# The causal mask as a matmul that opens each score bank of a four-layer decoder trunk

## The chip, the cores and the metric

The kernel runs on one core of one Trainium2 chip. The metric is the device time of one execution in microseconds (us); lower is better. One matrix engine (PE, the TensorE), three elementwise engines (DVE = VectorE, ACT = ScalarE, POOL = GpSimd) and the queue that issues transfers (SP) work side by side and wait for each other through semaphores. Scores and products land in PSUM, which has eight banks of 128 partitions x 512 float32.

## The reference

A trunk of four residual layers over 256 tokens of width 1024, batch 1. Layers 0 and 3 mix tokens by native sparse attention (NSA), layer 1 by block attention (MoBA), layer 2 by a gated short convolution; each layer ends in a dense SwiGLU network, and a last norm follows. With 256 tokens the sparse rules leave plain causal attention in two of NSA's three branches and in MoBA:

```python
def masked_softmax(s, mask):
    s = jnp.where(mask, s.astype(jnp.float32), -jnp.inf)
    m = jnp.max(s, axis=-1, keepdims=True)
    m = jnp.where(jnp.isfinite(m), m, 0.0)
    e = jnp.where(mask, jnp.exp(s - m), 0.0)
    d = jnp.sum(e, axis=-1, keepdims=True)
    return e / jnp.where(d > 0, d, 1.0)
...
# NSA: 16 heads, the selected and the window branch share the mask kpos <= t
o = (gates[:, :, 0] * o_cmp + gates[:, :, 1] * o_slc + gates[:, :, 2] * o_win) @ w_out
# MoBA: 16 heads, one block of 256 keys, mask kpos <= t
o = (masked_softmax(q @ k.T / 8, causal) @ v) @ w_out
```

## The kernel before

Activations stand with the model's width on the partitions, 256 tokens in the free dimension. All products are made from two parts of each number (high and low, type float32r), three matmuls for one product (`mm3`, L123 to L125). The weights stream from memory in blocks of 128x1024; `split_part` turns each into its parts (L104 the high one, L105 the low one), on ACT, DVE and POOL by a table. A projection (`project`) gathers 24 matmuls of 256 columns in one PSUM bank, and `scaled` (L276, DVE) multiplies it by the norm's factors.

Attention works by pairs of heads, eight pairs to a layer; the order of its steps is written out by hand (`NSA_ORDER`, `MOBA_ORDER`): q and k/K project, s makes scores and softmax, T transposes the probabilities (PE against an identity, then `split` on ACT and DVE, L138 and L139), P weighs the values. The framework's planner takes that order as a priority, and places an instruction earlier where its inputs and buffers allow it; on each engine the planned order is then fixed. PSUM is shared out by tags: A has four banks (projections, scores, values, output products), B three, C one.

`scores` of NSA fills three A banks for a pair: one with the first 128 queries of both heads and both branches (four blocks of 128x128, L643), and one for each head with the second 128 queries (two blocks of 128x256, L646). MoBA fills two (L371 to L373: two blocks of 128x128, two of 128x256). `softmax` (L297 to L314) is called once for each head in NSA and once for each pair in MoBA, with four score blocks each: for each block one DVE instruction (L306) reads the scores from PSUM, adds the mask, scales, writes the result to the SBUF tile `pr` and keeps the row's minimum, and a small read of that accumulator follows; ACT takes the exponential in place in `pr` (L309) with the row's sum, again with a small accumulator read; DVE makes the reciprocal of four sums (L311); POOL scales each block (L313). `pr` tiles hold 768 columns, and there are four of them.

The mask is a constant tile of 128x256 that is loaded at the start (L772) on the SP queue, behind the input and the first four weight blocks.

Of the kernel before, what the change touches and what calls it, by code (L numbers as in the profile page):

```python
# [51 lines left out]
class Kernel:  # L52
# [67 lines left out]
    def mm3(self, out, wt, act, first, last):  # L120
        """out += wt.T @ act, both as (high, low)."""
        mm = self.nc.tensor.matmul
        mm(out, wt[0], act[0], start=first, stop=False)  # L123
        mm(out, wt[0], act[1], start=False, stop=False)  # L124
        mm(out, wt[1], act[0], start=False, stop=last)  # L125

    def group(self, outs, acts):
        """outs[i][128, 256] = (weight tiles i, i + len(outs), ...).T @ acts."""
        n = len(acts)
        for k, a in enumerate(acts):  # L130
            if k == n - 1 and self.sums is None:
# [10 lines left out]
    def prep(self, k, norm):  # L142
        """The k-th slice of the norm's input: its parts times the gain, and its squares."""
# [130 lines left out]
    def scaled(self, p):  # L274
        f = self.row()
        self.nc.vector.tensor_tensor(out=f, in0=p, in1=self.rb, op=OP.mult)  # L276
        return f

    def values(self, at, put):
        """Token-major values of 512 columns; put(token tile, bank)."""  # L280
# [16 lines left out]
    def softmax(self, cols, gates):  # L297
# [3 lines left out]
        mn = self.sb([P, 4], "mn", bufs=3)  # L301
        den = self.sb([P, 4], "den", bufs=3)
        rc = self.sb([P, 4], "rc", bufs=3)
# [21 lines left out]
    def put_keys(self, dst, p):  # L325
        """dst[:, part, half, :]: the keys of a pair of heads, each with zeros for the other's rows."""
        nc = self.nc
        f = self.scaled(p)
# [10 lines left out]
    def moba(self, norm):  # L339
# [24 lines left out]
        def scores(p):  # L364
            q, kt = qs[p], self.keys[p % 4]
            s = []
            for t in range(NT):
                n = (t + 1) * P
                o = self.bank("A")[:, :2 * n].rearrange("p (a s) -> p a s", a=2)
                c = slice(t * P, (t + 1) * P)  # L370
                mm(o, q[:, 0, c], kt[:, 0, :, :n], start=True, stop=False)  # L371
                mm(o, q[:, 1, c], kt[:, 0, :, :n], start=False, stop=False)
                mm(o, q[:, 0, c], kt[:, 1, :, :n], start=False, stop=True)  # L373
                s.append(o)
            cols = [(s[t][:, i], slice((t + i) * S if t else i * P, (t + i + 1) * S if t else (i + 1) * P))
                    for t in range(NT) for i in range(2)]
            prs.append(self.softmax(cols, [1.0] * 4))

        def turn(p):
            pr = prs[p]  # L380
            b0, b1 = self.bank("B"), self.bank("B")
            for i in range(2):
                nc.tensor.transpose(b0[:, i * S:i * S + P], pr[:, i * P:(i + 1) * P], self.ident)
                o = (1 + i) * S
                nc.tensor.transpose(b0[:, i * S + P:(i + 1) * S], pr[:, o:o + P], self.ident)
                nc.tensor.transpose(b1[:, i * P:(i + 1) * P], pr[:, o + P:o + S], self.ident)
# [27 lines left out]
    def nsa(self, j, norm):  # L414
# [7 lines left out]
        # Keys and values to compress: rows (l % 2, d), the lower half one token ahead.  # L422
# [18 lines left out]
        def put_blocks(n):  # L441
            """Parts of the blocks' rows l = 2 jj, 2 jj + 1; columns (part, group, block), the position as block 15."""
# [15 lines left out]
        # Keys of the other branches: kk[:, part, branch, :], each part on both halves.  # L458
        def put_keys(b, gp):
            def put(p):  # L460
                f = self.scaled(p)
# [21 lines left out]
        # Queries: per head high and low parts on the two halves.  # L483
# [19 lines left out]
        def compress(n):  # L503
            """Rows (part, group, block), columns hidden."""
# [34 lines left out]
        def compress_keys(_):  # L539
            """Compressed keys on both halves."""  # L540
# [8 lines left out]
        def compress_values(_):  # L549
            """Compressed values as rows (r, part, block), one block of rows for each head of a group."""  # L550
# [27 lines left out]
        def compressed(gp):  # L578
            """Probabilities of the compressed blocks for 8 heads, rows (r, part, block)."""
# [42 lines left out]
        def put_values(t, p):  # L622
            """Per branch and pair of groups: (group, high | low | high, d)."""
# [13 lines left out]
        def scores(p):  # L637
            kk = self.keys[p // 2]
            s0 = self.bank("A").rearrange("p (i b s) -> p i b s", i=2, b=2)
            s1 = [self.bank("A").rearrange("p (b s) -> p b s", b=2) for _ in range(2)]  # L640
            for i in range(2):
                for n in range(2):
                    mm(s0[:, i], qs[p][:, i, :P], kk[:, n, :, :P], start=(n == 0), stop=(n == 1))  # L643
# [3 lines left out]
            prs.append([])  # L647
            for i in range(2):
                cols = [(s0[:, i, b], slice(b * P, (b + 1) * P)) for b in range(2)]
                cols += [(s1[i][:, b], slice((1 + b) * S, (2 + b) * S)) for b in range(2)]  # L650
                h = 2 * p + i
                g = [gates[:, t, 16 * (b + 1) + h:16 * (b + 1) + h + 1] for t in range(2) for b in range(2)]
                prs[p].append(self.softmax(cols, g))
# [94 lines left out]
    def run(self):  # L748
# [23 lines left out]
        self.mask = load("mask", [P, S])  # L772
# [4 lines left out]
        make_identity(nc, self.ident)  # L777
        self.ones = const.tile([P, 1], F32, tag="ones", name="ones")
# [38 lines left out]
def wide_tiles(w, cols):  # L817
    """[K, cols] -> tiles ordered (k, column block)."""
# [4 lines left out]
def stream():  # L823
    """The weights in the order of use: (step, array, layer of its kind, columns or rows of them)."""
# [37 lines left out]
def tiles(x):  # L862
    """The stream as blocks of PART tiles side by side."""
# [12 lines left out]
def layout(x):  # L876
    t = np.arange(S)
    own = np.where(np.arange(P)[:, None] >= np.arange(P)[None, :], 0.0, NEG)
    mask = np.concatenate([np.zeros((P, P)), own], axis=1).astype(np.float32)
# [35 lines left out]
```

## Time and profile before

| what | us |
|---|---|
| median of three runs | 1336.04 |
| lowest and highest run | 1332.56, 1336.41 |
| span of the profiled execution, first to last instruction | 1335.3 |
| PE busy | 1275.1 |
| DVE busy | 958.5 |
| ACT busy | 680.1 |
| POOL busy | 322.1 |

The profile shows the span of its execution, and no time around it; the span is 0.7 us under the median of the runs. A busy time counts an engine's instructions from start to end, overlaps once; matmuls overlap, and a matmul's row is longer than its step to the next one.

### The profile page before, as it was taken

The numbers are of one execution on the slowest core, as the hardware profiler recorded it, in microseconds if no ns is written. First come the engines' busy times: TensorE is split into PE (matmuls) and PEld (weight loads), VectorE is DVE, ScalarE is ACT, GpSimd is POOL, SyncE is SP. The second block draws the span as 40 slices with busy tenths as digits, with TensorE's granted clock in tenths as the row PEclk, the third lists the DMA queues.
The fourth block names the chain that finished last, engine by engine and source line by source line (L and its number), as shares of the span: only waits on it lengthen the run. The fifth ranks groups of instructions, "written<-read, shape, count | busy, mean of one in ns | idle before, by whom it ended". The sixth has DMA issues, their size and how long they took to land.

```text
span 1335.3 us, 25478 instructions
## 1 busy us (share of the span) xinstructions
PE 1275.1 (95%) x10064; PEld 1239.5 (93%) x10064; DVE 958.5 (72%) x1726; ACT 680.1 (51%) x1297; POOL 322.1 (24%) x341
## 2 busy tenths in 40 slices
PE   7779999999999899999999999999997989999997
PEld 7778899999989899999999999999996779999997
DVE  7988877665658886666658777665679798766642
ACT  4759845444434545444434344444346796544442
POOL 5457630000256320000113120000333666000010
PEclk9889999999999999999999999999998899999999
DMA  6443066555554236656555556666546312656651
GB/s 225 150 160 111 18 190 187 179 187 184 179 175 152 101 122 195 180 184 187 177 189 173 191 174 190 178 186 187 178 142 213 103 48 77 193 183 182 188 178 60
DMA packets 60744, 215.52 MB, mean 161 GB/s; under 512 B 7248, under 2 KB 7632, under 8 KB 60624
## 3 DMA queue, kind: packets, MB, share of 16 engines
q1 hardware_dynamic: 60480, 213.85, 50.9%
q8 instruction: 79, 1.29, 0.4%
q14 instruction: 41, 0.34, 0.1%
q10 hardware_dynamic: 144, 0.04, 0.0%
HBM read 212.81 MB, written 1.05 MB: 160 GB/s over the span
## 4 chain that ended last, share of the span: by engine, by line
PE 78%; DVE 13%; ACT 4%; issue 3%; DMA 1%; POOL 0%; POOLq 0%; DVEq 0%; ACTq 0%
PE psA L123 22%; PE psA L124 22%; PE psA L125 22%; DVE wlo L105 2%; PE psB L123 2%; PE psB L124 2%; PE psB L125 2%; ACT pr L309 1%; DVE ff L139 1%; DVE pt L139 1%; DVE row L276 1%; PE psA L289 1%; DVE pr L306 1%; PE psA L290 1%; PE psA L291 1%
## 5 line engine op out<-in xcount | busy, mean ns | idle before, releaser
L105 DVE TENSOR_TENSOR wlo<-raw,whi 128x1024 fp32r<-128x1024 f32 (+1 forms) x351 | 430.8, 1231 | 186.4 <-ACT whi L104 185.4
L123 PE MATMUL psA<-at,whi 128*128 128x256 f32 x1896 | 541.6, 286 | 18.1 <-DVE row L276 11.4
L104 ACT CAST whi<-raw 128x1024 fp32r<-128x1024 f32 (+1 forms) x372 | 386.0, 1040 | 335.5 <-issue 131.8
L125 PE MATMUL psA<-at,wlo 128*128 128x256 f32 x1896 | 539.9, 285 | 4.7 <-DVE wlo L105 2.8
L124 PE MATMUL psA<-at,whi 128*128 128x256 f32 x1896 | 539.4, 284 | 0.0
L123 PEld LDWEIGHTS psA<-at,whi 128*128 128x128 f32 x1896 | 366.5, 193 | 19.8 <-ACT whi L104 7.2
L125 PEld LDWEIGHTS psA<-at,wlo 128*128 128x128 f32 x1896 | 366.5, 193 | 6.2 <-DVE wlo L105 4.2
L124 PEld LDWEIGHTS psA<-at,whi 128*128 128x128 f32 x1896 | 366.7, 193 | 0.4
L124 PE MATMUL psA<-ff,whi 128*128 128x256 f32 x840 | 236.7, 282 | 2.1 <-DVE ff L139 2.1
L123 PE MATMUL psA<-ff,whi 128*128 128x256 f32 x840 | 236.7, 282 | 0.0
L125 PE MATMUL psA<-ff,wlo 128*128 128x256 f32 x840 | 236.0, 282 | 0.0
L167 POOL TENSOR_TENSOR ssq<-ssq,row 128x256 f32<-128x256 f32 x54 | 54.8, 1015 | 592.8 <-issue 476.7
L124 PEld LDWEIGHTS psA<-ff,whi 128*128 128x128 f32 x840 | 158.2, 188 | 2.8 <-DVE ff L139 2.5
L123 PEld LDWEIGHTS psA<-ff,whi 128*128 128x128 f32 x840 | 158.1, 188 | 0.1
L125 PEld LDWEIGHTS psA<-ff,wlo 128*128 128x128 f32 x840 | 158.0, 188 | 0.0
L105 POOL TENSOR_TENSOR wlo<-raw,whi 128x1024 fp32r<-128x1024 f32 (+1 forms) x55 | 133.2, 2427 | 77.8 <-ACT whi L104 37.1
L138 ACT CAST ff<-row 128x256 fp32r<-128x256 f32 x120 | 48.8, 407 | 127.9 <-DVE row L245 96.1
L139 DVE TENSOR_TENSOR ff<-row,ff 128x256 fp32r<-128x256 f32 x120 | 65.1, 543 | 37.7 <-ACT ff L138 36.7
L269 DVE TENSOR_TENSOR gu<-psA,rb 128x512 f32<-128x512 f32 x80 | 55.2, 691 | 38.5 <-PE psA L125 38.4
L313 POOL TENSOR_SCALAR pr<-pr,rc,gates 128x256 f32<-128x256 f32 (+1 forms) x128 | 69.3, 556 | 40.5 <-DVE rc L311 33.1
L309 ACT ACTIVATE pr<-pr,mn 128x128 f32<-128x128 f32 (+1 forms) x160 | 71.3, 449 | 6.1 <-DVE mn L306 5.7
L165 ACT ACTIVATE row<-h 128x256 f32<-128x256 f32 x63 | 24.5, 413 | 68.9 <-DVE h L229 67.3
(192 smaller groups left out, 1582.8 us busy)
## 6 DMA issues: line engine op xcount, KB each, us to landing
raw<-in_w SPq DMA_DIRECT2D x400, 512.0 KB, 3.6
h<-in_xt SPq DMA_DIRECT2D x4, 256.0 KB, 5.1
raw<-in_w SPq DMA_DIRECT2D x4, 256.0 KB, 5.2
out<-ff SPq DMA_DIRECT2D x4, 256.0 KB, 2.5
w<-in_w SPq DMA_DIRECT2D x2, 256.0 KB, 4.3
mask<-in_mask SPq DMA_DIRECT2D x1, 128.0 KB, 7.0
cneg<-in_cneg SPq DMA_DIRECT2D x1, 128.0 KB, 6.7
cone<-in_cone SPq DMA_DIRECT2D x1, 128.0 KB, 5.7
```

Source lines behind the costliest of these rows:

```text
L104: copy(hi[:, c], src[:, c])
L105: eng.tensor_tensor(out=lo[:, c], in0=src[:, c], in1=hi[:, c].bitcast(F32), op=OP.subtract)
L123: mm(out, wt[0], act[0], start=first, stop=False)
L124: mm(out, wt[0], act[1], start=False, stop=False)
L125: mm(out, wt[1], act[0], start=False, stop=last)
L138: self.nc.scalar.copy(dst[:, 0], src)
L139: self.nc.vector.tensor_tensor(out=dst[:, 1], in0=src, in1=dst[:, 0].bitcast(F32), op=OP.subtract)
L165: nc.scalar.activation(sq, h, AF.Square)
L167: nc.gpsimd.tensor_tensor(out=self.ssq, in0=self.ssq, in1=sq, op=OP.add)
L269: nc.vector.tensor_tensor(out=gu, in0=p, in1=self.rb[:, None, :].to_broadcast([P, 2, S]), op=OP.mult)
L309: nc.scalar.activation(pr[:, c], pr[:, c], AF.Exp, bias=mn[:, j:j + 1], scale=-1.0, accum_out=den[:, j:j + 1])
L313: nc.gpsimd.tensor_scalar(pr[:, c], pr[:, c], rc[:, j:j + 1], gates[j], op0=OP.mult, op1=OP.mult)
```

## The change

The mask tile becomes 128x128 and of the other sign (0 where a key is seen, 3.0e38 where it isn't). It is loaded to a scratch row and copied as float32r (`maskr`), and so is the identity (`identr`): two copies on ACT at the start. Before the score matmuls of a bank, one matmul of `identr` with `maskr`, repeated n times, opens the bank and writes the mask to the diagonal blocks; the score matmuls then all add. The keys are scaled by -1/8 when they are made (one DVE instruction with two multiplications in place of one with one), so the row's minimum is that of the negated scores. In `softmax` one DVE reduction takes the minima of all blocks of a bank, and ACT takes the exponential from PSUM and writes `pr`. NSA's softmax is called once for a pair: one reciprocal for eight (or, in MoBA, four) sums. MoBA has two `pr` tiles for a pair where it had one; there are still four tiles.

```diff
-    def scaled(self, p):
+    def scaled(self, p, scale=None):
         f = self.row()
-        self.nc.vector.tensor_tensor(out=f, in0=p, in1=self.rb, op=OP.mult)
+        if scale is None:
+            self.nc.vector.tensor_tensor(out=f, in0=p, in1=self.rb, op=OP.mult)
+        else:
+            self.nc.vector.scalar_tensor_tensor(f, p, scale, self.rb, op0=OP.mult, op1=OP.mult)
         return f
...
+    def masked(self, bank, t, n):
+        out = bank[:, :n * (t + 1) * P].rearrange("p (n s) -> p n s", n=n)[:, :, t * P:]
+        self.nc.tensor.matmul(out, self.identr, self.maskr[:, None, :].to_broadcast([P, n, P]), start=True, stop=False, skip_group_check=True)
+
+    def softmax(self, banks):
         nc = self.nc
-        pr = self.sb([P, 3 * S], "pr", bufs=PR_BUFS)
...
-        for j, (src, c) in enumerate(cols):
-            n = c.stop - c.start
-            nc.vector.tensor_tensor_reduce(pr[:, c], src, self.mask[:, S - n:], -QSCALE, 3.0e38, OP.add, OP.min,
-                                           mn[:, j:j + 1])
-        for j, (src, c) in enumerate(cols):
-            nc.scalar.activation(pr[:, c], pr[:, c], AF.Exp, bias=mn[:, j:j + 1],
-                                 scale=-1.0, accum_out=den[:, j:j + 1])
+        prs = [self.sb([P, 3 * S], "pr", bufs=PR_BUFS) for _ in range(2)]
...
+        for s, where in banks:
+            k = s.shape[1]
+            nc.vector.tensor_reduce(out=mn[:, o:o + k], in_=s, op=OP.min, axis=AX.X)
+            for x in range(k):
+                j, (i, c, g) = o + x, where[x]
+                nc.scalar.activation(prs[i][:, c], s[:, x, :], AF.Exp, bias=mn[:, j:j + 1],
+                                     scale=-1.0, accum_out=den[:, j:j + 1])
+                todo.append((prs[i][:, c], j, g))
+            o += k
         nc.vector.reciprocal(rc, den)
-        for j, (src, c) in enumerate(cols):
-            nc.gpsimd.tensor_scalar(pr[:, c], pr[:, c], rc[:, j:j + 1], gates[j], op0=OP.mult, op1=OP.mult)
-        return pr
+        for x, j, g in todo:
+            nc.gpsimd.tensor_scalar(x, x, rc[:, j:j + 1], g, op0=OP.mult, op1=OP.mult)
+        return prs
...
# MoBA scores, for t in range(2)
-                o = self.bank("A")[:, :2 * n].rearrange("p (a s) -> p a s", a=2)
+                bank = self.bank("A")
+                self.masked(bank, t, 2)
+                o = bank[:, :2 * n].rearrange("p (a s) -> p a s", a=2)
-                mm(o, q[:, 0, c], kt[:, 0, :, :n], start=True, stop=False)
+                mm(o, q[:, 0, c], kt[:, 0, :, :n], start=False, stop=False, skip_group_check=True)
...
# NSA scores
+            b0, b1 = self.bank("A"), [self.bank("A") for _ in range(2)]
+            self.masked(b0, 0, 4)
...
             for i in range(2):
+                self.masked(b1[i], 1, 2)
                 for n in range(2):
-                    mm(s1[i], qs[p][:, i, P:], kk[:, n], start=(n == 0), stop=(n == 1))
+                    mm(s1[i], qs[p][:, i, P:], kk[:, n], start=False, stop=(n == 1), skip_group_check=True)
...
+            prs.append(self.softmax(banks))
...
# run
-        self.mask = load("mask", [P, S])
+        mask = self.row()[:, :P]
+        nc.sync.dma_start(mask, ap["mask"])
...
+        self.identr = const.tile([P, P], F32R, tag="identr", name="identr")
+        nc.scalar.copy(self.identr, self.ident)
+        self.maskr = const.tile([P, P], F32R, tag="maskr", name="maskr")
+        nc.scalar.copy(self.maskr, mask)
```

## Rows read from the trace of the kernel before

**Rows 1.** The page, busy time of PE and the chain that ended last, by engine.
```profile
PE 1275.1 (95%) x10064; PEld 1239.5 (93%) x10064; DVE 958.5 (72%) x1726; ACT 680.1 (51%) x1297; POOL 322.1 (24%) x341
...
PE 78%; DVE 13%; ACT 4%; issue 3%; DMA 1%; POOL 0%; POOLq 0%; DVEq 0%; ACTq 0%
```

**Rows 2.** Windows: stretch, its us, then busy us by engine, granted clock, DMA.
```profile
85.00:165.00 80.00, 74.43 (x489) 64.17 (x489) 67.66 (x243) 69.11 (x211) 58.18 (x80) 0.99 0.21 70
400.00:480.00 80.00, 73.94 (x544) 69.14 (x543) 67.71 (x165) 42.42 (x126) 36.69 (x41) 0.98 0.36 115
1040.00:1125.00 85.00, 77.94 (x507) 67.74 (x507) 69.49 (x232) 69.01 (x206) 56.55 (x69) 0.97 0.21 66
```

**Rows 3.** Chain by line, shares of 85 to 165, 400 to 480, 1040 to 1125.
```profile
by line: DVE pt L139 6.7%; DVE pr L306 5.3%; ACT pr L309 4.6%; PE psC L681 4.6%; DVE ff L139 4.4%; PE psA L125 4.1%; ACT pt L138 4.0%; PE psA L123 4.0%; PE psA L124 3.8%; ACT whi L104 3.8%; PE psA L646 3.7%; DVE ff L494 3.2%; DVE row L693 3
...
by line: issue 9.6%; PE psA L125 7.6%; PE psA L124 7.6%; PE psA L123 7.5%; DVE whi L104 7.4%; DVE ff L139 6.2%; ACT pr L309 4.8%; DVE row L276 4.3%; DVE wlo L105 4.3%; DVE pt L139 4.1%; POOL pr L313 3.6%; DVE keys L332 2.8%; DVE pr L306 2.7
...
by line: ACT pr L309 14.1%; DVE ff L139 7.4%; DVE pt L139 7.1%; issue 6.1%; DVE row L693 4.6%; DVE pr L306 4.2%; ACT pt L138 3.5%; ACT gu L690 3.3%; DVE ff L494 3.3%; PE psB L584 2.8%; ACT whi L104 2.8%; PE psA L646 2.7%; PE psC L681 2.5%; 
```

**Rows 4.** Timeline of PE, 117 to 123: start, us, what, count.
```profile
117.47 0.64 PE L643 MATMUL psA<-keys,ff 128*128 128x256 f32 x4
117.94 1.09 PE L646 MATMUL psA<-keys,ff 128*128 128x512 f32 x4
118.87 0.27 PE L662 MATMUL psB<-ident,pr 128*128 128x128 f32 x1
...
121.56 0.63 PE L686 MATMUL psC<-pt,ff 128*128 128x256 f32 x4
122.03 0.40 PE L688 MATMUL psC<-ptc,ff 128*128 128x256 f32 x2
```

**Rows 5.** Timeline of DVE, 129 to 131, score blocks back to back.
```profile
129.34 0.28 DVE L306 CUSTOM_DVE_ANT_0 pr<-psA,mask 128x128 f32<-128x128 f32 x1
...
129.76 0.42 DVE L306 CUSTOM_DVE_ANT_0 pr<-psA,mask 128x256 f32<-128x256 f32 x1
...
130.45 0.28 DVE L306 CUSTOM_DVE_ANT_0 pr<-psA,mask 128x128 f32<-128x128 f32 x1
```

**Rows 6.** Timeline of DVE, 136 to 141, a reduction and its successor.
```profile
137.04 0.41 DVE L596 TENSOR_REDUCE cmx<-row 128x16 f32<-128x256 f32 x1
137.37 0.17 DVE L311 RECIPROCAL rc<-den 128x4 f32<-128x4 f32 x1
```

**Rows 7.** Groups by line and shape: busy us, mean ns of one, idle before.
```profile
L269 DVE TENSOR_TENSOR gu<-psA,rb 128x512 f32<-128x512 f32 x80 | 55.2, 691 | 38.5 <-PE psA L125 38.4
L138 ACT CAST ff<-row 128x256 fp32r<-128x256 f32 x120 | 48.8, 407 | 127.9 <-DVE row L245 96.1 <-DVE row L733 15.0 <-DVE row L276 14.8
L276 DVE TENSOR_TENSOR row<-psA,rb 128x256 f32<-128x256 f32 x46 | 18.7, 416 | 1.2 <-PE psA L125 0.7
L311 DVE RECIPROCAL rc<-den 128x4 f32<-128x4 f32 x40 | 6.9, 172 | 6.4 <-POOL pr L313 3.1 <-ACT pr L309 3.0
L727 DVE SCALAR_TENSOR_TENSOR row<-gu,cw,row 128x256 f32<-128x256 f32 x8 | 3.9, 483 | 0.2
L138 ACT CAST pt<-psB 128x256 fp32r<-128x256 f32 x8 | 3.0, 376 | 0.5 <-PE psB L386 0.5
```

**Rows 8.** Timelines of ACT and POOL: exponentials of pair six, scalings of pair seven.
```profile
146.21 0.40 ACT L309 ACTIVATE pr<-pr,mn 128x128 f32<-128x128 f32 x1 [0.34 <-DVE mn L306]
...
147.99 0.39 ACT L309 ACTIVATE pr<-pr,mn 128x128 f32<-128x128 f32 x1
...
149.25 0.49 ACT L309 ACTIVATE pr<-pr,mn 128x256 f32<-128x256 f32 x1
...
1108.50 3.88 POOL L313 TENSOR_SCALAR pr<-pr,rc,gates 128x128 f32<-128x128 f32 x8 [2.13 <-DVE rc L311]
```

**Rows 9.** The start: the mask's issue, its time to landing, ACT's timeline.
```profile
6.19 0.47 SPq L769 DMA_DIRECT2D mask<-in_mask  x1
...
mask<-in_mask SPq DMA_DIRECT2D x1, 128.0 KB, 7.0
...
12.86 1.14 ACT L104 CAST whi<-raw 128x512 fp32r<-128x512 f32 x2 [1.98 <-DMA raw<-in_w]
```

More of the change, by code (lines that the diff above doesn't have):

```diff
@@ L295, in values @@
             put(t, p)
-    def softmax(self, cols, gates):
+    def masked(self, bank, t, n):
+        out = bank[:, :n * (t + 1) * P].rearrange("p (n s) -> p n s", n=n)[:, :, t * P:]
+        self.nc.tensor.matmul(out, self.identr, self.maskr[:, None, :].to_broadcast([P, n, P]), start=True, stop=False, skip_group_check=True)
+    def softmax(self, banks):
         nc = self.nc
-        pr = self.sb([P, 3 * S], "pr", bufs=PR_BUFS)
-        mn = self.sb([P, 4], "mn", bufs=3)
-        den = self.sb([P, 4], "den", bufs=3)
-        rc = self.sb([P, 4], "rc", bufs=3)
-        for j, (src, c) in enumerate(cols):
-            n = c.stop - c.start
-            nc.vector.tensor_tensor_reduce(pr[:, c], src, self.mask[:, S - n:], -QSCALE, 3.0e38, OP.add, OP.min,
-                                           mn[:, j:j + 1])
-        for j, (src, c) in enumerate(cols):
-            nc.scalar.activation(pr[:, c], pr[:, c], AF.Exp, bias=mn[:, j:j + 1],
-                                 scale=-1.0, accum_out=den[:, j:j + 1])
+        prs = [self.sb([P, 3 * S], "pr", bufs=PR_BUFS) for _ in range(2)]
+        n = sum(s.shape[1] for s, _ in banks)
+        mn = self.sb([P, 8], "mn", bufs=3)[:, :n]
+        den = self.sb([P, 8], "den", bufs=3)[:, :n]
+        rc = self.sb([P, 8], "rc", bufs=3)[:, :n]
+        o, todo = 0, []
+        for s, where in banks:
[7 more added lines that the diff above has]
+            o += k
         nc.vector.reciprocal(rc, den)
-        for j, (src, c) in enumerate(cols):
-            nc.gpsimd.tensor_scalar(pr[:, c], pr[:, c], rc[:, j:j + 1], gates[j], op0=OP.mult, op1=OP.mult)
-        return pr
+        for x, j, g in todo:
+            nc.gpsimd.tensor_scalar(x, x, rc[:, j:j + 1], g, op0=OP.mult, op1=OP.mult)
+        return prs
     def steps(self, order, does):
@@ L327, in put_keys @@
         nc = self.nc
-        f = self.scaled(p)
+        f = self.scaled(p, -QSCALE)
         for i in range(2):
@@ L368, in scores @@
                 n = (t + 1) * P
-                o = self.bank("A")[:, :2 * n].rearrange("p (a s) -> p a s", a=2)
+                bank = self.bank("A")
+                self.masked(bank, t, 2)
+                o = bank[:, :2 * n].rearrange("p (a s) -> p a s", a=2)
                 c = slice(t * P, (t + 1) * P)
-                mm(o, q[:, 0, c], kt[:, 0, :, :n], start=True, stop=False)
[L372 to L377, printed above, removed]
+                mm(o, q[:, 0, c], kt[:, 0, :, :n], start=False, stop=False, skip_group_check=True)
+                mm(o, q[:, 1, c], kt[:, 0, :, :n], start=False, stop=False, skip_group_check=True)
+                mm(o, q[:, 0, c], kt[:, 1, :, :n], start=False, stop=True, skip_group_check=True)
+                s.append((o, [(i, slice(t * P, (t + 1) * P + t * P), 1.0) for i in range(2)]))
+            prs.append(self.softmax(s))
         def turn(p):
-            pr = prs[p]
             b0, b1 = self.bank("B"), self.bank("B")
[L382 to L386, printed above, removed]
+            for i, pr in enumerate(prs[p]):
+                nc.tensor.transpose(b0[:, i * S:i * S + P], pr[:, :P], self.ident)
+                nc.tensor.transpose(b0[:, i * S + P:(i + 1) * S], pr[:, P:S], self.ident)
+                nc.tensor.transpose(b1[:, i * P:(i + 1) * P], pr[:, S:S + P], self.ident)
             t0 = self.sb([P, 2, 512], "pt", F32R, bufs=PT_BUFS)
@@ L460, in put @@
             def put(p):
-                f = self.scaled(p)
+                f = self.scaled(p, -QSCALE)
                 for i in range(2):
@@ L638, in scores, with gate @@
             kk = self.keys[p // 2]
-            s0 = self.bank("A").rearrange("p (i b s) -> p i b s", i=2, b=2)
-            s1 = [self.bank("A").rearrange("p (b s) -> p b s", b=2) for _ in range(2)]
+            b0, b1 = self.bank("A"), [self.bank("A") for _ in range(2)]
+            self.masked(b0, 0, 4)
+            s0 = b0.rearrange("p (i b s) -> p i b s", i=2, b=2)
+            s1 = [x.rearrange("p (b s) -> p b s", b=2) for x in b1]
             for i in range(2):
                 for n in range(2):
-                    mm(s0[:, i], qs[p][:, i, :P], kk[:, n, :, :P], start=(n == 0), stop=(n == 1))
+                    mm(s0[:, i], qs[p][:, i, :P], kk[:, n, :, :P], start=False, stop=(n == 1), skip_group_check=True)
             for i in range(2):
+                self.masked(b1[i], 1, 2)
                 for n in range(2):
-                    mm(s1[i], qs[p][:, i, P:], kk[:, n], start=(n == 0), stop=(n == 1))
-            prs.append([])
-            for i in range(2):
[L649 to L653, printed above, removed]
+                    mm(s1[i], qs[p][:, i, P:], kk[:, n], start=False, stop=(n == 1), skip_group_check=True)
+            def gate(t, b, i):
+                h = 2 * p + i
+                return gates[:, t, 16 * (b + 1) + h:16 * (b + 1) + h + 1]
+            banks = [(b0.rearrange("p (n s) -> p n s", n=4),
+                      [(i, slice(b * P, (b + 1) * P), gate(0, b, i)) for i in range(2) for b in range(2)])]
+            for i in range(2):
+                banks.append((s1[i], [(i, slice((1 + b) * S, (2 + b) * S), gate(1, b, i)) for b in range(2)]))
+            prs.append(self.softmax(banks))
         prs, pend, outs = [], [], []
@@ L878, in layout @@
     own = np.where(np.arange(P)[:, None] >= np.arange(P)[None, :], 0.0, NEG)
-    mask = np.concatenate([np.zeros((P, P)), own], axis=1).astype(np.float32)
+    mask = -own.astype(np.float32)
     ends = np.arange(16) * 16 + 31
```

## Prediction

> **What bounds the kernel now.** I read the page first: PE is busy 95% of the span, and the chain that ended last lies on PE for 78% [rows 1]. Taken over the whole span that says "a kernel bound by its matmuls". The change touches only the stretches in which scores are made, so the second view is the table of windows over them: 85 to 165 us (layer 0), 400 to 480 (MoBA), 1040 to 1125 (layer 3). The reader should see that PE is still at 93, 92 and 92% there, but not alone: DVE has 85, 85 and 82%, ACT 86, 53 and 81% [rows 2]. PE stands still for 5.6 + 6.1 + 7.1 = 18.7 us of these 245. The third view is the chain inside each window [rows 3]: no engine owns it. Of the shares that the first row lists in full (52%), PE's lines have 20, which is 39%; in the second 23 of 73 (31%); in the third 8 of 64 (12%). The lines that the change edits stand high: L306 has 5.3, 2.7 and 4.2%, which is 4.2 + 2.2 + 3.6 = 10.0 us, L309 4.6, 4.8 and 14.1%, which is 3.7 + 3.8 + 12.0 = 19.5 us. So the score stretches are bound by latency handed from PE to DVE to ACT to POOL and back. DVE and ACT work saved there is worth a part of its size, and so is PE work added.
>
> **PE: mask matmuls.** A pair of NSA gets one of 512 columns and two of 256, a pair of MoBA two of 256. Steps: four L643 of 256 columns fill 117.47 to 117.94, 0.118 each; four L646 of 512 fill 117.94 to 118.87, 0.23 each [rows 4]. So 0.466 a pair in NSA and 0.236 in MoBA: 16 x 0.466 + 8 x 0.236 = 9.3 us of new PE work. Its bounds on the path are nothing (they need neither queries nor keys, only a free bank, and 18.7 us stand idle) and 9.3 (all in line). The planner may place one early, where PE waits; but a free A bank usually comes just before the scores are due, and in the projections of MoBA PE has no gaps. I take PE's share of the chain, about 40%: **+3.7**.
>
> Two of three mask matmuls in NSA, and one of two in MoBA, write two runs of 128 columns with a gap. L686 writes just so, and four of them fill 121.56 to 122.03, the step of L643 [rows 4]; I add nothing.
> [...]
>
> **DVE: minima.** Before, two blocks of 128 take 129.34 to 129.76, 0.21 each, two of 256 take 129.76 to 130.45, 0.345 each, accumulator reads included [rows 5]. A pair of NSA is 4 x 0.21 + 4 x 0.345 = 2.22, one of MoBA 1.11. After: a reduction of 256 columns has a step of 0.33 (137.04 to 137.37) [rows 6]; one of 512 from PSUM doesn't occur. From below: 128 columns more cost 0.135 in L306 [rows 5], so 0.33 + 0.27 = 0.60. From above: the whole row of L269, which also reads 512 columns of PSUM, 0.69 [rows 7]. I take 0.60, since the rows of one engine overlap at their ends. A pair of NSA then costs 1.80, one of MoBA 0.93: 16 x 0.42 + 8 x 0.18 = 8.2 us less of 44.4 (18%). Sixteen reciprocals of 0.172 go as well, 2.7. The sixteen key scalings grow from 0.416 (L276) to at most 0.483 (L727, the nearest form) [rows 7], 1.0 more. Net 9.9 us less DVE work, 4.8 with reductions of 0.69. On the path: 18% of L306's 10.0 us, and a little for reciprocals: **-2.1** (bounds 0 and -9.9).
>
> **ACT: exponentials from PSUM.** Same number, same columns; only the source moves. The nearest pair is L138 on 256 columns, 407 ns from SBUF and 376 from PSUM [rows 7]: 31 ns less, 160 times, 5.0 us (bounds 0 and 5). One exponential has a step of (149.25 - 146.21) / 7 = 0.43 [rows 8], so 7% of L309's 19.5 us: **-1.4**.
> [...]
>
> **What waits longer.** (a) One reciprocal for a pair: before, the first head's four exponentials end near 147.9 and POOL can scale it while ACT does the second head; now POOL starts only after all eight, (149.25 - 147.99) + 0.49 = 1.75 us later [rows 8]. POOL's eight scalings take 3.88 us in line and it already waits 2.13 for the reciprocal [rows 8]. For most pairs projections or output products cover this on PE; at the end of an NSA layer the cover thins out and up to 1.75 is open, twice. I take 0.6 a layer: **+1.2** (bounds 0 and 6). (b) An A bank is free after its exponentials, not after its minima. NSA's scores take three of four A banks, and queries, values and output products queue behind them. A pair's exponentials take 149.25 + 0.49 - 146.21 = 3.5 us [rows 8], and pairs follow each other by 10 us in the mean (eight in 80), so this is mostly covered: **+0.7** (0 to 4). (c) MoBA's four `pr` tiles hold two pairs, not four. In the written order only the fourth scores step runs with three pairs before it unturned or being turned, so its exponentials wait for one transpose; a projection of 24 matmuls, 24 x 0.118 = 2.8 us, covers it: **+0.3** (0 to 2). (d) The start: ACT's copy of the mask waits for the transfer, issued at 6.19 and 7.0 on its way, so until 13.2. In the planned order it may stand in ACT's gap of 1.98 before the cast at 12.86 [rows 9], or ahead of a weight cast on which PE waits: **+0.3** (0 to 4). The identity's copy falls into the first us, while ACT waits for the input. The mask's transfer is halved; it was off the path. The `pr` scratch row taken for the mask is freed before the last of seven is wanted.
>
> **Sum.** +3.7 - 2.1 - 1.4 + 1.2 + 0.7 + 0.3 + 0.3 = +2.7 us on the profiled 1335.3, 1338.0; the runs' median lies 0.7 above that span, so **1338.7**.
>
> **Rivals.** *PE in line* (0.25): PE is full enough that mask matmuls go one behind another on its path, all 9.3, with 1 us of savings showing: 1344 to 1347. For it: 93% busy [rows 2]. Against: 18.7 us idle, and the masks don't wait for data. *Relief wins* (0.25, the other side): mask matmuls slip into PE's idle time, and DVE and ACT, which hold the chain of layer 3 [rows 3], pass on half of their 9.9 + 5.0: -7.4, and up to 2.5 of the waits stays: 1328 to 1331. It decides if more than half of the masks are issued before their queries are ready. Against: only about 20% of L306 is saved, and PE's lines hold a third of the first two windows. *Late hand-over* (0.10): the joined reciprocal and the held banks reach their bounds by half or more, 5 to 10 us in place of the 1.9 taken: 1342 to 1347. For it: layer 3's chain is ACT's [rows 3]; against: ten us from pair to pair. *Slow mask matmuls* (0.03): the 40 with a gap in their output run at half pace, 40 x 0.118 = 4.7 more: 1343.
> [...]
>
> **How the numbers follow.** My own forecast (0.37) has its own range of 1333 to 1341; it ends around even, since a new plan of 25,000 instructions alone can move a stretch by a us or two. A measurement of this kernel can tell about 0.3%, 4 us, from no change. Faster is the second rival, 0.25; slower the other three, 0.38; the same 0.37. Leaving one in ten out on each side gives 1329 to 1347.
>
> **What will show it.** Right: PE's busy time up by 7 to 9 us; 64 mask matmuls with steps of 0.12 and 0.23; the new reduction near 0.69 long; L309's counterpart 20 to 45 ns shorter; POOL's longest wait for the reciprocal up by 1 to 2 us; the FFN stretches unchanged. The step to fail first is the 40%: if mask matmuls stand in PE's idle time, the kernel is faster than I say; if PE's idle time in the three windows stays at 18 us or grows, slower. If ACT stands before 13 us on the mask, (d) was wrong.

## The result and the profile after

The changed kernel takes 1354.34 us in the median of four runs (1351.35 to 1357.75), the kernel before, on the same chip, 1336.22 (1332.56 to 1336.87). The ratio is 1.0143, its 95% interval 1.0122 to 1.0164: slower by 16 to 22 us, and outside the forecast range. The profiled execution has a span of 1351.7, 16.4 more than before.

The page of the changed kernel, busy time; it answers to [rows 1]:
```profile
PE 1284.5 (95%) x10128; PEld 1248.2 (92%) x10128; DVE 953.3 (71%) x1454; ACT 675.5 (50%) x1299; POOL 318.0 (24%) x341
```
PE has 64 matmuls and 9.4 us more, as forecast; its idle time grew as well, from 1335.3 - 1275.1 = 60.2 to 1351.7 - 1284.5 = 67.2. So the 16.4 are 9.4 of more busy time and 7.0 of more idle time. DVE and ACT have less work, and nothing of that is seen in the time.

Where it went can be read between the nine places at which POOL makes a norm's factor (L193). Layer 0's attention took 175.8 us (168.1 before), MoBA 128.7 (124.0), layer 3's attention 170.1 (165.8). Conv and the four FFN stretches are as before to 0.1, the start is 0.2 shorter. So the loss is +7.7, +4.7 and +4.3, all of it where scores are made. Times by layer, here and below, come from one execution of each kernel, and its share of lower clock moves them by a few us (last section).

Groups of the changed kernel by line and shape; they answer to the steps of [rows 4 to 8]:
```profile
L317 DVE TENSOR_REDUCE mn<-psA 128x2 f32<-128x512 f32 x40 | 26.8, 682 | 6.4 <-PE psA L660 6.3
L317 DVE TENSOR_REDUCE mn<-psA 128x2 f32<-128x256 f32 x8 | 3.3, 411 | 0.5 <-PE psA L388 0.5
L279 DVE SCALAR_TENSOR_TENSOR row<-psA,rb 128x256 f32<-128x256 f32 x16 | 6.7, 419 | 0.5 <-PE psA L125 0.4
L320 ACT ACTIVATE pr<-psA,mn 128x256 f32<-128x256 f32 x80 | 37.3, 481 | 7.8 <-DVE mn L317 7.7
L320 ACT ACTIVATE pr<-psA,mn 128x128 f32<-128x128 f32 x80 | 28.7, 370 | 5.6 <-DVE mn L317 5.2
L326 POOL TENSOR_SCALAR pr<-pr,rc,gates 128x128 f32<-128x128 f32 x64 | 31.5, 505 | 47.8 <-DVE rc L324 35.9 <-DVE ff L582 11.7
```
The exponentials of the kernel before:
```profile
L309 ACT ACTIVATE pr<-pr,mn 128x256 f32<-128x256 f32 x80 | 40.0, 501 | 4.0 <-DVE mn L306 3.7
L309 ACT ACTIVATE pr<-pr,mn 128x128 f32<-128x128 f32 x80 | 31.5, 396 | 2.1 <-DVE mn L306 1.9
```
The single prices were right. The reduction of 512 columns is 682 ns long (two of them in 1.28, a step of 0.60), the key scaling cost 419 ns where up to 483 was allowed, the exponentials are 481 and 370 ns long where L309 had 501 and 396. None of that explains 18 us. What is left is the added matmuls, and the waits.

Waits of PE in the changed kernel, the rows that are new or longer: us in total, times, longest.
```profile
PE psA L123 <- DVE row L277: 16.1, 4, 5.1
PE psB L680 <- POOL pr L326: 6.8, 7, 1.6
...
PE psA L123 <- ACT pr L320: 1.9, 1, 1.9
...
PE psB L395 <- POOL pr L326: 1.7, 1, 1.7
```
The rows that answer to them in the kernel before:
```profile
PE psA L123 <- DVE row L276: 11.4, 3, 5.3
...
PE psB L385 <- POOL pr L313: 1.0, 3, 0.5
PE psB L663 <- POOL pr L313: 0.9, 4, 0.3
...
PE psB L383 <- POOL pr L313: 0.5, 1, 0.5
```
Before, PE's transposes waited 2.4 for POOL in all, and it waited for no A bank behind an exponential. The fourth wait of the changed kernel's first row stands in layer 3, behind the first pair's scores; the kernel before has two shorter ones there. The changed kernel, then the kernel before:
```profile
1045.83 0.58 PE L123 MATMUL psA<-at,whi 128*128 128x256 f32 x1 [4.95 <-DVE row L277]
```
```profile
1028.98 0.36 PE L123 MATMUL psA<-at,whi 128*128 128x256 f32 x1 [0.49 <-DVE mn L306]
...
1034.62 0.81 PE L643 MATMUL psA<-keys,ff 128*128 128x256 f32 x4 [2.54 <-DVE row L276]
```
Before, the next projection got its bank behind a minimum (L306), and PE could run it before it stood still. Experiment 4, which only lets the exponentials read PSUM, has one wait of 4.22 there too, experiment 3, which only joins the reciprocal, 0.49 and 1.59. That points to the kept banks; but experiment 2, which keeps none, also stands 4.14 there behind a minimum, so the place answers to added matmuls as well.

One place shows the late hand-over from end to end. The changed kernel's layer 0, PE's and DVE's timelines (start, us, what, and in brackets the idle time before and its releaser):
```profile
141.31 0.33 PE L679 MATMUL psB<-ident,pr 128*128 128x128 f32 x1 [0.34 <-POOL pr L326]
...
143.36 0.37 PE L680 MATMUL psB<-ident,pr 128*128 128x128 f32 x1 [1.60 <-POOL pr L326]
...
145.02 0.42 PE L679 MATMUL psB<-ident,pr 128*128 128x128 f32 x1
145.23 0.42 PE L680 MATMUL psB<-ident,pr 128*128 128x128 f32 x1
...
145.52 0.56 PE L304 MATMUL psA<-maskr,identr 128*128 128x256 f32 x1
145.88 1.05 PE L660 MATMUL psA<-keys,ff 128*128 128x512 f32 x2
```
```profile
142.44 0.68 DVE L317 TENSOR_REDUCE mn<-psA 128x4 f32<-128x512 f32 x1
143.04 0.29 DVE L612 TENSOR_SCALAR cmx<-cmx 128x16 f32<-128x16 f32 x1
146.97 0.69 DVE L317 TENSOR_REDUCE mn<-psA 128x2 f32<-128x512 f32 x1 [3.64 <-PE psA L660]
```
and POOL's, of the changed kernel and then of the kernel before, at the like place:
```profile
140.81 4.10 POOL L326 TENSOR_SCALAR pr<-pr,rc,gates 128x128 f32<-128x128 f32 x8
```
```profile
140.54 1.98 POOL L313 TENSOR_SCALAR pr<-pr,rc,gates 128x128 f32<-128x128 f32 x4 [0.30 <-DVE rc L311]
143.55 2.45 POOL L313 TENSOR_SCALAR pr<-pr,rc,gates 128x128 f32<-128x128 f32 x4 [1.03 <-DVE rc L311]
```
Before, POOL got head 0's four scalings (1.98 us) while ACT was at head 1's exponentials. Now all eight come in one run of 4.10 us, bank by bank, so that head 0's two wide stretches are scaled fifth and sixth. PE reaches the transpose of the first of them at 141.76 and stands for 1.60. Behind that transpose, in PE's order, are the next pair's mask matmuls and scores; so DVE runs dry for 3.64 us, and ACT after it (2.16 us at 146.8). In the 10 us from 140 PE, DVE and ACT are busy 6.79, 6.07 and 6.85 in the changed kernel; in the kernel before 8.34, 9.43 and 8.49:
```profile
140.00:150.00 10.00, 6.79 (x32) 5.34 (x30) 6.07 (x16) 6.85 (x26) 7.10 (x15) 0.83 0.00 1
```
```profile
140.00:150.00 10.00, 8.34 (x54) 6.91 (x54) 9.43 (x49) 8.49 (x33) 6.21 (x13) 1.00 0.00 1
```

### The profile page after: what moved, and what is told of

Same layout as the page of the kernel before. It is cut to its first block, busy times and chain, and to the rows that moved or that the text cites. A ratio compares the mean times of both kernels' runs of the same rounds, so it can differ in the third digit from the quotient of the medians.

```text
span 1351.7 us, 25364 instructions
## 1 busy us (share of the span) xinstructions
PE 1284.5 (95%) x10128; PEld 1248.2 (92%) x10128; DVE 953.3 (71%) x1454; ACT 675.5 (50%) x1299; POOL 318.0 (24%) x341
## 5 line engine op out<-in xcount | busy, mean ns | idle before, releaser
L123 PE MATMUL psA<-at,whi 128*128 128x256 f32 x1896 | 544.3, 287 | 25.4 <-DVE row L277 16.1
L105 DVE TENSOR_TENSOR wlo<-raw,whi 128x1024 fp32r<-128x1024 f32 (+1 forms) x351 | 434.1, 1240 | 188.6 <-ACT whi L104 186.8
L123 PEld LDWEIGHTS psA<-at,whi 128*128 128x128 f32 x1896 | 369.1, 195 | 27.6 <-DVE row L277 10.3
L123 PE MATMUL psA<-ff,whi 128*128 128x256 f32 x840 | 237.1, 283 | 0.0
L123 PEld LDWEIGHTS psA<-ff,whi 128*128 128x128 f32 x840 | 158.3, 188 | 0.5
L105 POOL TENSOR_TENSOR wlo<-raw,whi 128x1024 fp32r<-128x1024 f32 (+1 forms) x55 | 130.7, 2383 | 91.7 <-ACT whi L104 44.8
L139 DVE TENSOR_TENSOR ff<-row,ff 128x256 fp32r<-128x256 f32 x120 | 68.5, 571 | 38.0 <-ACT ff L138 37.6
L326 POOL TENSOR_SCALAR pr<-pr,rc,gates 128x128 f32<-128x128 f32 (+1 forms) x128 | 69.7, 559 | 47.8 <-DVE rc L324 35.9
L320 ACT ACTIVATE pr<-psA,mn 128x128 f32<-128x128 f32 (+1 forms) x160 | 65.6, 426 | 13.4 <-DVE mn L317 13.0
```

The lines of the kernel that those rows point to most:

```text
L105: eng.tensor_tensor(out=lo[:, c], in0=src[:, c], in1=hi[:, c].bitcast(F32), op=OP.subtract)
L320: nc.scalar.activation(prs[i][:, c], s[:, x, :], AF.Exp, bias=mn[:, j:j + 1], scale=-1.0, accum_out=den[:, j:j + 1])
L326: nc.gpsimd.tensor_scalar(x, x, rc[:, j:j + 1], g, op0=OP.mult, op1=OP.mult)
```

## The experiments

The theory after the result: the loss is a later hand-over, from two parts (the reciprocal joined over a pair; A banks kept until their exponentials are done), with the mask matmuls on top. Its rivals: the mask matmuls are all of it (they stand in PE's line); or MoBA's fewer live pairs are. Times are medians; before was 1335.24 to 1336.64 in the runs beside them. A ratio's distance from 1 is turned into us by 1336.

**1. Opening matmuls on the kernel before, of zeros** (b_open): +19.8 us.
```
+out = bank[:, :n * (t + 1) * P].rearrange("p (n s) -> p n s", n=n)[:, :, t * P:]
+zero = self.zk[:, 0, :DH]
+self.nc.tensor.matmul(out..., self.zk[:, 0, :P],
+                      zero...to_broadcast([P, n, 2, DH]), start=True, stop=False, ...)
```


> The kernel before, with one thing added: a matmul of zeros opens each score bank, with the shapes and places of the mask matmuls; masks, minima, exponentials and reciprocals stay as before. If the 64 matmuls stand in line on PE's path: +9 us (ratio 1.007), PE busy +9.3. If they fit into PE's idle time: 0 to +3 us (1.000 to 1.002). If opening a bank early starves the projections of A banks: more than +10.

Measured: 1354.92, ratio 1.0148 (1.0132 to 1.0165). This run doesn't price the matmuls. Its zeros came from `zk`, which the compression of the keys writes, so the first scores of each NSA layer had to wait for that step. It lands in the expected case of more than 10, but not for its reason, a projection that finds no bank. Its waits of PE show what that did:
```profile
PE psB L552 <- DVE row L544: 20.2, 2, 11.3
```
Two waits, 20.2 us in all; the kernel before has 0.2 there. MoBA, which nothing of that touches, took 123.6 us (124.0 before). That doesn't show that the opening matmuls were hidden there, since its granted clock was 1.00 where the kernel before has 0.99 over 124 us (about 1.7 us, as an estimate by windows of 1 us); the next run has 1.1 more there.

**2. The same work without the wait** (b_open2): +6.1 us. The operands are those of the score product that follows and overwrites the result.
```
+mm(o[:, :, t * P:], q[:, 0, c], kt[:, 0, :, t * P:n], start=True, stop=True)
 mm(o, q[:, 0, c], kt[:, 0, :, :n], start=True, stop=False)
...
+mm(s0, qs[p][:, 0, :P], kk[:, :, :, :P], start=True, stop=True)
...
+mm(s1[i][:, :, P:], qs[p][:, i, P:], kk[:, 0, :, P:], start=True, stop=True)
```


> The kernel before, with 64 added matmuls of the mask matmuls' shapes and output patterns (16 of 512 columns, 48 of 256), each made of the operands that the score product behind it reads, which overwrites it. So nothing waits for anything new, and only TensorE's work grows, by about 9 us. Theory that the mask matmuls stand in TensorE's line: +8 to +10 us (1344 to 1346). Theory that TensorE's idle time takes up most of them and that the new waits make the loss: +0 to +4 us (1335 to 1340).

Measured: 1342.38, ratio 1.0046 (1.0030 to 1.0063), so 4.0 to 8.4 us. PE's busy time went up by 5.1 only (1280.2), though the added matmuls have the steps of 0.12 and 0.23; it isn't exact to better than some us (with no matmul added, experiment 6's a_nomask has 1277.0, 1.9 over the kernel before, and experiment 8's b_quick 1281.8, 6.7 over it). The layers with scores went up by 2.5, 1.1 and 1.7. Both theories missed by a little: about two thirds of the 9.3 us show, neither all nor a few.

**3. The joined reciprocal alone, on the kernel before** (b_joint): +12.4 us.
```
+den = self.sb([P, 8], "den", bufs=3)
+rc = self.sb([P, 8], "rc", bufs=3)
+for i, (cols, gates) in enumerate(heads):
+    ...
+nc.vector.reciprocal(rc, den)
+for x, k, g in todo:
+    nc.gpsimd.tensor_scalar(x, x, rc[:, k:k + 1], g, op0=OP.mult, op1=OP.mult)
```


> The kernel before, with NSA's two reciprocals of a pair joined into one of eight sums; everything else as before. Theory 'the joined reciprocal hands over late': +5 to +8 us, nearly all in layers 0 and 3 (about +4 and +2), with PE's transposes waiting for POOL some 10 us in all in place of 2. Rival 'masks and banks cost it all': within 2 us of before.

Measured: 1347.54, ratio 1.0093 (1.0077 to 1.0110). Sixteen fewer reciprocals, no other work added, and two thirds of the changed kernel's loss; more than the 5 to 8 expected. Layers: +6.4, -0.2 and +2.5; MoBA, where a softmax was always one pair, doesn't move. Its waits of PE, and POOL's timeline in layer 0:
```profile
PE psB L687 <- POOL pr L317: 6.5, 13, 0.6
```
```profile
142.35 4.08 POOL L317 TENSOR_SCALAR pr<-pr,rc,gates 128x128 f32<-128x128 f32 x8 [3.23 <-DVE rc L315]
149.62 0.69 POOL L317 TENSOR_SCALAR pr<-pr,rc,gates 128x128 f32<-128x128 f32 x1 [3.20 <-DVE rc L315]
```
POOL now waits 3.2 us twice for a reciprocal and then works 4.08 in one run, where it had 0.30 and 1.03 before; PE's transposes wait for it 13 times.

**4. Kept banks alone, on the kernel before** (b_hold): +6.8 us.
```
-nc.scalar.activation(pr[:, c], pr[:, c], AF.Exp, bias=mn[:, j:j + 1], scale=-1.0, ...)
+nc.scalar.activation(pr[:, c], src, AF.Exp, bias=mn[:, j:j + 1], scale=QSCALE, ...)
```


> The kernel before, only that each exponential reads the scores in PSUM instead of the minimum's result in SBUF (it leaves the mask out of the exponentials). So a bank is held until its exponentials are done; the minima, the reciprocal for each head and TensorE's work are those of before. Theory that held banks are a main cause of the loss: 1341 to 1346. Theory of the joined reciprocal: banks are there in time, and the shorter exponentials give what the prediction took: 1333 to 1337.

Measured: 1342.40, ratio 1.0051 (1.0035 to 1.0067). Only the source of the exponentials moved; each is shorter, and the kernel is slower. The waits of PE say why:
```profile
PE psA L123 <- DVE row L276: 14.1, 4, 4.7
...
PE psA L646 <- ACT pr L309: 4.0, 5, 0.9
...
PE psA L123 <- ACT pr L309: 2.4, 3, 2.0
```
Scores (L646) and projections (L123) wait for a bank behind an exponential, 6.4 us in 8 waits, none of which the kernel before has. One of 2.0 is in MoBA, before a projection, and stands there in the changed kernel too (its 1.9 above).

**5. Both** (b_hold_joint): +9.6 us.

> The same with the reciprocal joined over a pair of NSA heads: the changed kernel's hand-over without its mask matmuls and its joined minima (the mask is left out of the exponentials). If the joined reciprocal is the cause and held banks cost nothing: as the joined reciprocal alone, 1346 to 1349. If held banks add: 1350 or more. If both only uncover the same idle time: as the changed kernel without mask matmuls, 1347 to 1350, whichever of the two comes first.

Measured: 1345.44, ratio 1.0072 (1.0059 to 1.0084). The two don't add (6.8 and 12.4 alone), and together they cost less than the joined reciprocal alone. That they make the same hand-over late, and that the exponentials' shorter time works against it, is argued. The clock is a part of it: by the estimate of the last section the joined reciprocal alone lost up to 5.6 us to a lower clock, the kept banks 1.8, both together 0.7.

**6. The changed kernel without mask matmuls** (a_nomask): +12.7 us against before, 6.4 less than the changed kernel.
```
-self.masked(b0, 0, 4)
...
-mm(s0[:, i], ..., start=False, ...)
+mm(s0[:, i], ..., start=(n == 0), ...)
```


> The changed kernel without its 64 mask matmuls; it leaves out the causal mask, all else is as in the changed kernel. Theory that the mask matmuls stand in TensorE's line: 1344 to 1346. Theory of the late hand-over (reciprocal joined over a pair, banks held by the exponentials): 1348 to 1353, as most of the loss is in what stays. If the rest of the change were worth a gain, as the prediction's rival of relief had it: under 1336.

Measured: 1348.58, ratio 1.0095 (1.0078 to 1.0112). That kernel keeps the whole relief of DVE and ACT and has PE's work of before, and it is still 10 to 15 us slower than before. So mask matmuls are a third of the loss, from this side (6.4) as from the other (6.1), and the rest lies in what stays, the softmax. (The 6.4 is a difference of two ratios, taken beside different runs; by their intervals it is uncertain by some 3.6.)

**7. A reciprocal for each head again, in the changed kernel.** Three forms: exponentials head by head (a_split, +23.4), exponentials in the order of the banks (a_split2, +15.9), and this one without the mask matmuls (a_split2_nomask, +8.1).
```
+def close(side):
+    nc.vector.reciprocal(rc[side], den[side])
+    for x, y, g in todo_of[side]:
+        nc.gpsimd.tensor_scalar(x, x, rc[side][:, y:y + 1], g, op0=OP.mult, op1=OP.mult)
...
-nc.vector.reciprocal(rc, den)
...
+    if k == 2 and len(todo_of[side]) == 4 and (sides == 1 or where[0][0] == side):
+        close(side)
```


> The changed kernel with a reciprocal for each head of an NSA pair again, the exponentials and scalings of one head ahead of the other's. Theory 'joined reciprocal': back by 5 to 7 us of the 18 (1347 to 1350). Rival 'masks and banks': within 2 us of the changed kernel, 1352 to 1356.

> The changed kernel with a reciprocal for each head of an NSA pair, now with the exponentials left in the order of the banks: head 0's reciprocal and its four scalings come right behind its third exponential step, ahead of head 1's last bank. Theory of the joined reciprocal: 6 to 9 us come back (1345 to 1348). Theory of mask matmuls and held banks: no change within 2 us (1352 to 1356).

> The changed kernel with a reciprocal for each NSA head, the exponentials in the order of the banks, and without the mask matmuls (it leaves out the causal mask). If mask matmuls and joined reciprocal are all of the loss: 1335 to 1340. If held banks or the order of the exponentials by bank cost by themselves: 1343 to 1348.

Measured: 1358.49 (1.0175, 1.0159 to 1.0191), 1352.33 (1.0119, 1.0099 to 1.0139) and 1344.27 (1.0061, 1.0048 to 1.0075). Without mask matmuls the split gives back 12.7 - 8.1 = 4.6 us and leaves the kernel where kept banks alone put it (6.8). With them it gives 3.2, within the intervals of the two; the 6 to 9 expected did not come. Head by head costs 4 more than the changed kernel itself, where 5 to 7 less were expected: there the bank that two heads share is read by head 1 after all of head 0; that this bank is then kept longer is argued, not measured.

**8. GpSimd's order, and its share.** Head 0's scalings first (a_order, +16.3); the eight scalings shared out between POOL and DVE (a_quick, +19.1, and a_split2_quick, with a reciprocal for each head, +18.2); one of four on DVE in the kernel before (b_quick, +16.7).
```
-for x, j, g in todo:
+for x, j, g, _ in sorted(todo, key=lambda w: w[3]):
...
-nc.gpsimd.tensor_scalar(x, x, rc[:, j:j + 1], g, ...)
+(nc.vector if x.shape[-1] == S else nc.gpsimd).tensor_scalar(x, x, rc[:, j:j + 1], g, ...)
```


> The changed kernel with one thing moved: GpSimd scales head 0's four stretches of a pair first and then head 1's, instead of bank by bank; the reciprocal stays joined. Theory that TensorE waits in line for head 0's last scaling (6.8 us in 7 waits in the changed kernel's trace): that scaling comes some 1.1 us earlier for each pair, and 3 to 6 us come back (1348 to 1351). If the joined reciprocal itself is late, or the mask matmuls are all of it: 1352 to 1356.

> The changed kernel, with the scalings of the second token tile's stretches (128x256, half of a pair's eight) on VectorE instead of GpSimd; the reciprocal stays joined. The step from reciprocal to last scaling falls from about 4.4 us to about 2 us for each NSA pair; VectorE gets some 22 us of new work (80 by about 0.28). Theory that the late hand-over of a pair is what holds TensorE: 4 to 8 us come back (1346 to 1350). If that hand-over is not on the path in the changed kernel, and mask matmuls and kept banks are all: 1353 to 1362, VectorE's new work on top.

> The same with a reciprocal for each head in the order of the banks: the shortest hand-over that the changed kernel can have with these engines. Theory of the late hand-over: 7 to 11 us come back against the changed kernel, so that only the mask matmuls and part of the kept banks stay (1343 to 1347). If mask matmuls and kept banks are all: 1352 to 1362.

> The kernel before, with the last of each softmax's four scalings (128x256) on VectorE: its hand-over is about 0.6 us shorter for each head, VectorE gets some 11 us more. If the hand-over binds the kernel before too, and VectorE has room: 1328 to 1333, faster than both kernels. If VectorE's full stretch by the end of the NSA layers takes it: 1336 to 1342.

Measured: 1352.80 (1.0122, 1.0108 to 1.0137), 1355.19 (1.0143, 1.0126 to 1.0161), 1353.62 (1.0136, 1.0114 to 1.0157), 1354.11 (1.0125, 1.0106 to 1.0144). The order moves PE's waits at L680 from 6.8 us to 4.0, but its median by 1.5, which the intervals don't tell from nothing; 3 to 6 had been expected. So that head 0's wide stretches are scaled fifth and sixth, as at 140.81 above, isn't shown to cost anything; the joined reciprocal of experiment 3 scales head 0 first as it is. Sharing out gains nothing, and its row shows one reason:
```profile
L326 POOL TENSOR_SCALAR pr<-pr,rc,gates 128x128 f32<-128x128 f32 x64 | 35.0, 558 | 62.1 <-DVE rc L324 48.6 <-DVE ff L582 8.0 <-DVE cmx L612 3.2
L326 DVE TENSOR_SCALAR pr<-pr,rc,gates 128x256 f32<-128x256 f32 x64 | 24.5, 435 | 0.7
```
DVE's scalings took 435 ns (514 in MoBA), 32 us of new work in its queue, where 22 had been assumed (80 by 0.28, the author's estimate; L535, L158 and L726 of the kernel before, near forms on DVE, are 290, 350 and 354 ns long); POOL's own grew from 505 to 558 ns. These two came out where the rival (the hand-over is not on the path) had put them, but with DVE's new work on top they don't tell the theories apart. The fourth answers a different question: 21 us of added DVE work cost the kernel before 16.7 us, far above both expectations, while the lighter minima and the 16 reciprocals less gave the changed kernel nothing back. The 16.7 isn't DVE's work alone: up to 7.5 of it, as an estimate, are a lower clock of PE (last section), and POOL's own scalings grew there too, from 504 to 556 ns.

**9. MoBA's live pairs.** One `pr` tile for a pair in the changed kernel (a_one), two in the kernel before (b_two).
```
-prs = [self.sb([P, 3 * S], "pr", bufs=PR_BUFS) for _ in range(2)]
+pr = self.sb([P, 3 * S], "pr", bufs=PR_BUFS)
+prs = [pr[:, i * 3 * P:(i + 1) * 3 * P] for i in range(2)]
```


> The changed kernel with one probability tile instead of two for each MoBA pair, so four pairs of them can be alive as before. If the fewer pairs alive cost the changed kernel's MoBA layer its 4.7 us: 1349 to 1351. If, as the kernel before with two tiles showed, their number does not matter: 1353 to 1356.

> The kernel before, with two pr tiles for a MoBA pair in place of one (four tiles in all, so two pairs in flight and not four); everything else as before. Theory 'MoBA loses its depth': +2 to +3 us, all between the second and the third FFN. Rival: within 1 us, and MoBA's excess of 2.8 us over its mask matmuls has another cause.

Measured: 1357.20 (1.0152, 1.0136 to 1.0169) and 1334.84 (0.9996, 0.9986 to 1.0006). The number of live pairs is not the cause; that rival falls.

No version beat the kernel before; two tiles in MoBA is level with it.

## Why the prediction was wrong, step by step

**The ladder.** From before, each rung adding a part: kept banks +6.8; minima and exponentials by bank, keys scaled on the way, the start +1.3 (not told from nothing); joined reciprocal +4.6; mask matmuls +6.4. Together 19.1. A rung is the difference of two runs, uncertain by about 3 us. The rungs depend on their order: the joined reciprocal put in first costs 12.4. By the estimate of the last section up to 2.1 of the 4.6 are a lower clock (3.9 in a_nomask, 1.8 in a_split2_nomask).

**What failed: terms (a) and (b).** The forecast gave the joined reciprocal 1.2 and the kept banks 0.7, since "ten us from pair to pair" and the projections behind would cover them. They cost 9.6 together (b_hold_joint, 7.9 to 11.2), with the relief of the exponentials already counted in. Both bounds had been named (6 and 4), and the rival of a late hand-over took 5 to 10 of them; its mechanism is the one found, at a chance of 0.10. Its range of 1342 to 1347 was still too low, as mask matmuls and relief were mis-sized as well (below). The reason for the low value was an average. A pair each 10 us in the mean says nothing of PE's order inside a pair: transposes stand ahead of the next pair's scores, so PE's wait for POOL starves DVE and ACT in turn (1.60, then 3.64 and 2.16 us at the place in layer 0), and the loop has no slack there, where it closes. [rows 8] had the sign of it: POOL waited 2.13 for the reciprocal and then worked 3.88 in line.

**(b) also missed where it waits.** It named queries, values and output products as queueing for NSA's banks, and let the mean of ten us cover them; MoBA it left out. In the traces a projection of MoBA waits 2.0 us behind an exponential, where I had counted on projections as cover, and one in layer 3 stands in the wait of 4.95 us.

**Mask matmuls.** Busy time came out right (9.4 for 9.3), in part by luck: between the changed kernel and the one without them it is 7.5, in experiment 2 5.1. On the path it is 6.1 to 6.4 by two pairs of kernels, for 3.7 forecast: two thirds in line where PE's share of the chain, 40%, was used (which the rows had for layer 0 alone; they had 31% and 12% for the other two). The idle time of PE was hardly used: only two of the 64, at 127.07 and 1091.45, have a gap behind them before PE's next work (1.46 and 1.43 us to its start). With this term alone the forecast would have been off by 2.6. The steps were 0.12 and 0.23 for 41 of the 64, as taken. Twenty took 0.07 to 0.11 more, some 1.8 us in all, and one ran at the lower clock. That surplus isn't the mask's: in the kernel before, 18 places among the score matmuls have it, also about 1.8 us in all, most of them first behind transposes, and in the changed kernel the score matmuls have next to none. One of them, in the kernel before, with a step of 0.32 in place of 0.23:
```profile
131.11 0.27 PE L664 MATMUL psB<-ident,pr 128*128 128x128 f32 x1
131.14 0.47 PE L646 MATMUL psA<-keys,ff 128*128 128x512 f32 x1
131.46 0.63 PE L643 MATMUL psA<-keys,ff 128*128 128x256 f32 x4
```
Runs with a gap cost nothing by themselves in this trace: the steps of the matmuls that write them are mostly 0.12 as well (at 74.33, 74.91 and 89.87, for instance), so the rival of slow mask matmuls falls. Its half pace, from which its 4.7 us follow, was the author's guess; no run shows it.

**Relief of DVE and ACT.** The steps were right: a reduction of 512 columns 0.60, an exponential 20 or 26 ns shorter for 31 taken. DVE's busy time fell by 5.2 us only, for 9.9, as other work on it grew (the 347 splits of 128x1024 at L105 by 3.9 us in all, the 120 of L139 from rows by 3.4). Of -2.1 and -1.4 that were to show, nothing did: the rung with the minima is +1.3. The kernel without mask matmuls has all of this relief and is 12.7 slower. A share of a chain was no measure of what a shorter step gives.

**Right.** The start (d): the start is no longer than before, and ACT copies the mask at 14.24 without standing on it. (The identity's copy was put into the first us; it is at 10.51, between two other pieces of work.) FFN and conv are unchanged. MoBA's two pairs (c) cost nothing (-0.5, interval -1.9 to 0.8).

**Open.** Undoing the joined reciprocal in the full changed kernel gives 3.2, within the error, where it gives 4.6 without mask matmuls; moving scalings to DVE could not settle it, as it loads DVE instead. So what the joined reciprocal costs inside the whole change is shown on its rungs only, not by taking it out of the changed kernel. And 2 of MoBA's 4.7 us are not put down to any part: mask matmuls have 1.9 (128.7 to 126.8 without them), kept banks 0.6, each from one execution; whose the wait of 1.7 for POOL at L395 is stays open too.

## What to carry to other kernels

When an edit joins two units of work into one instruction, count when the first half's consumer may start, and look up what stands behind that consumer on its engine; the instructions saved are the smaller number (here sixteen by 0.172, 2.7 us, against the 12.4 that b_joint lost). When an edit lets an engine read PSUM in place of SBUF, list everyone who takes banks from that pool, projections too: here the banks came free one engine later, and PE waited 6.4 us for them in 8 waits (b_hold). And where several engines stand at 81 to 93% in a ring, as in the two NSA layers here, price added work at two thirds or more (6.1 of 9.3 on PE, 16.7 of 21 on DVE) and saved work at nothing (the rung with the lighter minima is +1.3), until an experiment says otherwise.

## What was not expected of the hardware

PE's wait of 1.60 us in layer 0 cost more than its length, about 1.7 us more as an estimate: the granted clock behind it was 0.50. Windows of the changed kernel (stretch, its us, busy us of PE, PEld, DVE, ACT, POOL, granted clock):
```profile
142.00:143.00 1.00, 0.00 (x0) 0.00 (x0) 1.00 (x3) 1.00 (x6) 1.00 (x3) 1.00 0.00 0
143.00:144.00 1.00, 0.64 (x4) 0.51 (x5) 0.33 (x2) 0.97 (x5) 1.00 (x3) 0.75 0.00 0
143.50:145.50 2.00, 2.00 (x11) 1.83 (x11) 0.00 (x0) 1.10 (x4) 1.87 (x4) 0.50 0.00 0
145.50:147.00 1.50, 1.50 (x7) 1.31 (x6) 0.03 (x1) 1.26 (x3) 0.00 (x0) 0.53 0.00 0
```
After PE had stood still from 141.76 to 143.36, the granted clock was 0.50 to 0.53 until about 147. The ten transposes from 143.52 ran at a step of 0.21, where the same transposes at 152 to 154 in this trace have 0.11, and the scores behind them were late by that as well: about 1.7 us from 143.5 to 147, as an estimate from the two last rows (2.00 by 0.50 and 1.50 by 0.47). The kernel before keeps 1.00 through the like stretch, 140 to 150.

It doesn't follow that the clock made the loss. The mean granted clock of the profiled executions is 0.985 in both kernels, and the clock that wasn't granted in the three score layers, summed over windows of 1 us, comes to 6.8, 1.7 and 8.5 us before and 10.2, 1.7 and 5.1 us after: layer 0 lost 3.4 more, layer 3 as much less. In other runs it counts. Taken as (1 - granted clock) x span, mean of a kernel's runs less that of the kernel before beside it, it is 5.6 us of the 12 of b_joint, 1.8 of the 7 of b_hold, 0.7 of the 10 of b_hold_joint, 3.9 of the 12 of a_nomask, -0.6 for b_open2 and 7.5 of the 17 of b_quick. These are upper estimates, since PE isn't busy all the time at the lower clock. That PE's added waits are what lowers it there is argued; layer 0's place above is the one that shows the order of the two.

Exponentials from PSUM were shorter by 20 and 26 ns, but the accumulator reads behind them grew, 190 to 209 ns (160 of them).
